# Where the load of a modulation tile stands in the queue: behind the weights of the two steps that follow it, in place of ahead of them

## Chip, cores and metric

The kernel runs on one core of a Trainium2 chip. The metric is device time in microseconds (us) of one execution; lower is better. The kernel before took 1530.79 us, the median of three runs (1523.31, 1530.79 and 1536.02).

## What is computed

One decoder block on x of 256 tokens by 2048 channels, all in float32. Six vectors of 2048 (shifts, scales and gates) come from a conditioning vector c; they are what this document calls the modulation.

```python
mod = jax.nn.silu(c) @ w_mod + b_mod            # w_mod: 2048 x 12288
sh1, sc1, g1, sh2, sc2, g2 = jnp.split(mod, 6)
h = rms_norm(x, norm1_g) * (1.0 + sc1) + sh1
q, k, v, u, gates = jnp.split(h @ w_in, split_pts)
...                                             # causal attention over q, k, v; state-space scan over u
merged = sigmoid(gate_a) * (y_attn @ w_attn_br) + sigmoid(gate_s) * (y_ssm @ w_ssm_br)
x = x + g1 * (merged @ w_out)
h2 = rms_norm(x, norm2_g) * (1.0 + sc2) + sh2
up = causal_dwconv(h2 @ w_up, conv_w, conv_b)
val, gt = jnp.split(up, 2, axis=-1)
x = x + g2 * ((silu(gt) * val) @ w_down)
```

## The kernel before

All weights stream from HBM once, as tiles of 128 x 1024 float32 (512 KB), 656 of them. Three kinds of tile share the way in:

- **Weight tiles** (464). `split_hi` (line 186, ScalarE) rounds a landed tile to a high part `whi`, `split_lo` (line 191, VectorE) takes the rest `wlo`; TensorE then multiplies with both parts. One tile is one *step* of TensorE. The block functions `chan_block` (240), `tok_block` (331) and `joint_block` (284) append the steps: 24 matmuls of 256 columns, 12 of 512, or 8 of 512 with 8 of 256. The raw tile is done with when `wlo` has been written. There are three buffers each for `whi` and `wlo` (`WB = 3`), so the split of step n+2 can begin when TensorE has finished step n-1.
- **Modulation tiles for TensorE** (76, source `in_w_m`), read by `mod_block` (451). TensorE multiplies them raw, as float32, with the conditioning vector in 32 columns (line 464, written `modp`). The raw tile is done with when TensorE has read it. In most of the program they come two at a time; this document calls two of them a *unit*.
- **Gate tiles** (116, source `in_w_g`), read by `gate_block` (490): VectorE multiplies and sums them in one instruction (line 501). The raw tile is done with after that.

The order of the work is a list, `plan`, written by the block functions and by `with_mods` (988), which weaves units and gate tiles between the weight tiles at set rates. Around the steps spoken of below, it reads: weight, weight, unit of two modulation tiles, weight, gate tile, weight, gate tile. `go` (213) walks the list: for a weight it emits the splits up to two steps ahead (`split_ahead`), for a modulation or gate tile the reading instruction. TensorE's own order follows it: the unit's matmuls stand between the two weights' steps before them and the two behind.

All loads are issued from SyncE's queue (line 124, `load_next`), in the order of the list. The raw tiles of weights, modulation and gates share five buffers (`RAW = 5`, tile `raw`), taken in rotation: a load takes the buffer of the load five places before it, and SyncE's queue stands until that tile is done with. From line 1190 on (after about 610 us) modulation and gate tiles have four buffers of their own (`mraw`), and `raw` serves weights alone.

Stages by time in the profile: up to about 60 us the first loads and the norm; to about 320 us the input projection (`w_in`: tiles `up`, `kp`, `qp`, `vp`, `gep`) with the modulation of the first sub-layer; to about 440 us more of `w_in` without modulation tiles, and attention and scan; to about 600 us the gates (`gap`) and the attention branch (`pap`) with the modulation of the second; then the rest. The state-space scan and its tables run on VectorE and ScalarE beside all of this, a piece per step.

Of the kernel before, what the change touches and what calls it, by code (L numbers as in the profile page):

```python
# [42 lines left out]
def block_kernel(ctx: ExitStack, tc: tile.TileContext, I, out):  # L43
# [57 lines left out]
    R_SET, R_SCAN, R_QK, R_ATT = 0.9, 1.05, 2.0, 2.2  # L101
    R_LAST, R_GAP, R_PAP, R_GLU, R_PPP, R_OUT, R_FFN = 1.0, 1.3, 1.3, 0.6, 0.4, 0.9, 0.34
    plan = []
    loaded = []
    place = {"load": 0}

    ring = {"w": lambda: wp.tile([128, 2, 512], F32, name="raw", tag="raw", bufs=RAW)}

# [3 lines left out]
    def ring_of(i):  # L112
        return "mod" if plan[i][0] == "m" and "mod" in ring else "w"

    def load_next():
        kind, src, _ = plan[place["load"]]
        r = ring_of(place["load"])
        held[r] += 1
        raw = ring[r]()

        if r == "mod" and "lo" in place:
            V.tensor_copy(raw[:, 0, 0:1], place["lo"][:, 0, 0:1].bitcast(F32))
        flat = raw.rearrange("p a b -> p (a b)")
        DMA.dma_start(flat, src)
        loaded.append((raw, r))
        place["load"] += 1

    behind = {}

    def after(inst, earlier):  # L130

        tc.add_manual_dep(inst.ins, earlier.ins.name,
                          mybir.DependencyInfo(mybir.DependencyClass.NoSync, mybir.DependencyReason.DATA),
                          reason="order")
# [5 lines left out]
    def unload(i):  # L140
        held[loaded[i][1]] -= 1
        loaded[i] = None

    def load_ahead():
        while place["load"] < len(plan):
            r = ring_of(place["load"])
            if held[r] >= room[r]:
                break
            load_next()

    def load_until(i):
        while place["load"] <= i and place["load"] < len(plan):
            load_next()

    bg = []
    agenda = {}
# [2 lines left out]
    def later(n, fn):  # L159
        agenda.setdefault(clock["step"] + n, []).append(fn)  # L160
# [4 lines left out]
    def run_bg():  # L165
        for entry in list(bg):
            entry[2] += entry[1]
            while entry[2] >= 1.0:
                entry[2] -= 1.0
                if next(entry[0], None) is None:  # L170
                    bg.remove(entry)
                    break
# [25 lines left out]

    def add_weights(src, fn):
        weights.append(len(plan))  # L200
        plan.append(("w", src, fn))

    def add_mod(src, fn):
        plan.append(("m", src, fn))

    def split_ahead(n):
        while done["hi"] <= n + WB - 1 and done["hi"] < len(weights):
            load_until(weights[done["hi"]])
            split_hi(weights[done["hi"]])
            split_lo(weights[done["hi"]])  # L210
            done["hi"] += 1

    def go(end=None):

        while done["plan"] < (len(plan) if end is None else end):
            i = done["plan"]
            kind, _, fn = plan[i]
            if kind == "m":
                load_until(i)
                load_ahead()  # L220
                fn(loaded[i][0])
                unload(i)
                done["plan"] += 1
                continue
            split_ahead(weights.index(i, max(0, done["hi"] - 4)))
            load_ahead()
            fn(*hi_lo.pop(i))
            for f in agenda.pop(clock["step"], []):
                f()
            run_bg()  # L230
            clock["step"] += 1
            done["plan"] += 1
# [7 lines left out]
    def chan_block(name, w, c0, kbs, act_hi, act_lo, post, k0=0, w0=None, seed=None, groups=None):  # L240
# [39 lines left out]
        for u in range(kbs):  # L280
            add_weights(wsrc(w, (w0 if w0 is not None else k0 // 2) + u, c0),
                        lambda hi, lo, u=u: step(u, hi, lo))
# [168 lines left out]
    def mod_block(part, k0, nk, finish, ps_tile, lag=0):  # L451

        st = {}
        n = 128 * nk
        per = 1024 // n

        def step(kb, raw):
            if kb == 0:
                st["p"] = ps_tile([128, n], "modp")
            raw = raw.rearrange("p a b -> p (a b)").rearrange("p (k n) -> p k n", n=n)  # L460
            for i in range(per):
                k = per * kb + i
                r0 = 32 * (k % 4)
                mm = PE.matmul(st["p"][r0:r0 + 32], cpad[:, k], raw[:, i], start=k < 4, stop=k >= 12,  # L464
                               tile_position=(0, r0))
                if "mod" in behind:
                    after(mm, behind["mod"])
                behind["mod"] = mm
            if kb == 16 // per - 1:
                rows = sm.tile([128, n], F32, name="rows", tag="rows", bufs=RB)  # L470
                A.copy(rows, st["p"])
                if lag:
                    later(lag, lambda: finish(rows))
                else:
                    finish(rows)

        at = 32 * (0, 1, 3, 4).index(part) + 8 * (k0 // 4) + 2 * (k0 % 4)
        parts = [(I["w_m"][at + kb], lambda raw, kb=kb: step(kb, raw)) for kb in range(16 // per)]

        size = max(1, 4 // per)  # L480
        return [parts[i:i + size] for i in range(0, len(parts), size)]
# [8 lines left out]
    def gate_block(part, k0, nk, dst, done=None):  # L490

        st = {}
        base = 16 * (2, 5, 0, 3).index(part)

        def step(k, half, raw):
            flat = raw.rearrange("p a b -> p (a b)")
            if k == 0 and half == 0:
                st["s"] = sm.tile([128, nk, 2], F32, name="gsum", tag="gsum")
                V.tensor_copy(st["s"].rearrange("p a b -> p (a b)"), rb[:, 0:2 * nk])
            sums = st["s"]  # L500
            V.scalar_tensor_tensor(flat, flat, 1.0, cb[:, 1024 * half:1024 * half + 1024], op0=ALU.mult,  # L501
                                   op1=ALU.mult, accum_out=sums[:, k, half:half + 1])
            if k == nk - 1 and half == 1:
                ks = slice(k0, k0 + nk)
                V.tensor_add(dst[:, ks], sums[:, :, 0], sums[:, :, 1])
                V.tensor_add(dst[:, ks], dst[:, ks], b_mod[:, 16 * part + k0:16 * part + k0 + nk])
                if done is not None:
                    done()

        return [[(I["w_g"][base + k0 + k, half], lambda raw, k=k, half=half: step(k, half, raw))]  # L510
                for k in range(nk) for half in range(2)]
# [75 lines left out]
    def mod1(k0, nk):  # L587
        def sc(rows):
            cols_of(rows, 1, k0, nk, a1)
            scale_cols(a1, norm1_g, k0, nk)  # L590
            place["a1"] = k0

        def sh(rows):
            cols_of(rows, 0, k0, nk, sh1)
            make_h(k0, nk)

        if k0 == 0:
            return mod_block(1, k0, nk, sc, m1_tile) + mod_block(0, k0, nk, sh, bu_tile)
        return woven(mod_block(1, k0, nk, sc, m1_tile), gate_block(0, k0, nk, sh1, lambda: make_h(k0, nk)))
# [405 lines left out]
    def next_mod():  # L1005
        for part in mods.pop(0):
            add_mod(*part)
# [9 lines left out]
    chunks, k0 = [], 0  # L1017
# [4 lines left out]
    mods += m0[:len(m0) // 2]  # L1022
    all_mods()
    go()
    st1 = {}
    for q in range(8):
        squares(st1, range(2 * q, 2 * q + 2), xT[q])
    norm_rows(st1, a1[:, 0:1])
    mods += m0[len(m0) // 2:]
    all_mods()  # L1030
    go()
    set_gen = setup()
    spread(set_gen, R_SET)
# [51 lines left out]
    def mod2(j):  # L1085
        lag = int(j < 3)

        def sc(rows):
            cols_of(rows, 4, 4 * j, 4, a2)
            scale_cols(a2, norm2_g, 4 * j, 4)  # L1090

        scale = mod_block(4, 4 * j, 4, sc, m1_tile, lag)
        if j < 3:
            return woven(scale, gate_block(3, 4 * j, 4, sh2))
        return scale + mod_block(3, 4 * j, 4, lambda rows: cols_of(rows, 3, 4 * j, 4, sh2), bu_tile, lag)
# [107 lines left out]
    parts = [m for j in range(1, 4) for m in gate_block(2, 4 * j, 4, g1)]  # L1203
    while parts or rest:
        mods += parts[:4] + rest[:1]
        parts, rest = parts[4:], rest[1:]
# [209 lines left out]
```

## Time and profile before

| | |
|---|---|
| median of three runs | 1530.79 us |
| the profiled execution's own time | 1532.48 us |
| its span in the profile | 1530.6 us |
| TensorE (PE) busy | 1469.6 us, 96% |
| VectorE (DVE) busy | 1110.3 us, 73% |
| ScalarE (ACT) busy | 842.0 us, 55% |
| TensorE's granted clock, mean | 0.989 |
| moved by DMA | 353.47 MB, 231 GB/s in the mean |

PE stands for TensorE's matmuls and PEld for its weight loads, which overlap them; SPq is SyncE's queue, which only issues DMAs. In a row of waits, "A <- B" says that A stood idle until B was done. Matmul ends are modelled, and a matmul's shown duration overlaps the next one's, so a busy PE is not one at its peak.

### The profile page before, as it was taken

To read this page: it belongs to the slowest core of one execution; us is meant where nothing else is said; L and a number is where in the kernel's file an instruction comes from. 1 tells how busy PE (TensorE), PEld (TensorE's weight loads), DVE (VectorE), ACT (ScalarE), POOL (GpSimd) and SP (SyncE) were. 2 spreads that over 40 slices of the span, in tenths; PEclk is the share of its full clock that TensorE was granted. 3 is DMA by queue.
4 is the path that set the end of the run, shared out by engine and by line. 5 is a ranking of instruction groups with operands and counts; after the bars stand their busy time and mean duration, and the time that the engine had idled before them with its cause. 6 is when DMAs were issued, how large, how long until landed. Compare 5 with 4: busy or idle time off the path is not lost.

```text
span 1530.6 us, 24302 instructions
## 1 busy us (share of the span) xinstructions
PE 1469.6 (96%) x9382; PEld 1236.0 (81%) x9382; DVE 1110.3 (73%) x1881; ACT 842.0 (55%) x1193; POOL 9.8 (1%) x22
## 2 busy tenths in 40 slices
PE   7989989989999899999989999999999999999998
PEld 4757767689977678788868888888888888888887
DVE  2789765986676869999578888887555667666654
ACT  3665667867675534654445555555444455555442
POOL 1000000000000000000000000000000000000000
PEclk8999999999999999999999999999999999999999
DMA  8788878733357867879576777775555555555663
GB/s 298 283 292 298 297 267 293 244 125 125 127 192 274 286 253 273 326 244 344 188 274 235 250 264 245 255 257 201 191 187 189 191 192 188 189 189 191 205 209 110
DMA packets 99110, 353.47 MB, mean 231 GB/s; under 512 B 10962, under 2 KB 13138, under 8 KB 98994
## 3 DMA queue, kind: packets, MB, share of 16 engines
q1 hardware_dynamic: 97808, 348.17, 65.7%
q0 software_dynamic: 1040, 3.61, 0.7%
q8 instruction: 73, 1.20, 0.3%
q14 instruction: 43, 0.34, 0.1%
q10 hardware_dynamic: 146, 0.15, 0.0%
HBM read 349.79 MB, written 2.10 MB: 230 GB/s over the span
## 4 chain that ended last, share of the span: by engine, by line
PE 73%; DVE 10%; DMA 9%; ACT 5%; issue 3%; SPq 0%; ACTq 0%; DVEq 0%
PE vp L302 11%; PE dp L302 10%; PE gp L302 10%; PE dp L304 5%; PE vp L304 5%; PE gp L304 5%; DVE wlo L191 4%; PE outp L302 4%; DMA raw<-in_w_in_dram 3%; ACT whi L186 3%; PE gap L302 2%; PE outp L304 2%; PE modp L464 2%; PE ppp L302 2%; DMA raw<-in_w_ga_dram 2%
## 5 line engine op out<-in xcount | busy, mean ns | idle before, releaser
L191 DVE TENSOR_TENSOR wlo<-raw,whi 128x1024 fp32r<-128x1024 f32 x464 | 566.3, 1223 | 325.4 <-ACT whi L186 323.3
L186 ACT CAST whi<-raw 128x1024 fp32r<-128x1024 f32 x464 | 486.6, 1050 | 550.4 <-PE dp L302 131.8
L302 PE MATMUL vp<-hl,whi 128*128 128x512 f32 x704 | 244.9, 393 | 1.0 <-ACT whi L186 1.0
L302 PE MATMUL dp<-g,whi 128*128 128x512 f32 x704 | 244.3, 391 | 0.0
L302 PE MATMUL gp<-hl,whi 128*128 128x512 f32 x640 | 222.3, 392 | 0.0
L304 PE MATMUL dp<-g,wlo 128*128 128x256 f32 x704 | 197.7, 281 | 0.0
L304 PE MATMUL vp<-hl,wlo 128*128 128x256 f32 x704 | 196.1, 279 | 0.0
L304 PE MATMUL gp<-hl,wlo 128*128 128x256 f32 x640 | 178.2, 278 | 0.0
L302 PEld LDWEIGHTS vp<-hl,whi 128*128 128x128 f32 x704 | 131.9, 187 | 31.1 <-issue 1.3
L302 PEld LDWEIGHTS dp<-g,whi 128*128 128x128 f32 x704 | 131.9, 187 | 28.6
L302 PEld LDWEIGHTS gp<-hl,whi 128*128 128x128 f32 x640 | 119.8, 187 | 27.0
L304 PEld LDWEIGHTS dp<-g,wlo 128*128 128x128 f32 x704 | 133.0, 189 | 0.0
L304 PEld LDWEIGHTS vp<-hl,wlo 128*128 128x128 f32 x704 | 132.6, 188 | 0.0
L304 PEld LDWEIGHTS gp<-hl,wlo 128*128 128x128 f32 x640 | 120.6, 188 | 0.0
L302 PE MATMUL gap<-hl,whi 128*128 128x512 f32 x256 | 96.4, 415 | 0.8 <-ACT whi L186 0.8
L302 PE MATMUL outp<-m,whi 128*128 128x512 f32 x256 | 91.1, 400 | 0.0
L501 DVE SCALAR_TENSOR_TENSOR raw<-raw,cb 128x1024 f32<-128x1024 f32 x60 | 73.0, 1220 | 10.7 <-DMA raw<-in_w_g_dram 9.2
L304 PE MATMUL gap<-hl,wlo 128*128 128x256 f32 x256 | 73.9, 289 | 4.5 <-DVE wlo L191 4.5
L501 DVE SCALAR_TENSOR_TENSOR mraw<-mraw,cb 128x1024 f32<-128x1024 f32 x56 | 68.2, 1221 | 12.6 <-DMA mraw<-in_w_g_dram 12.0
L304 PE MATMUL outp<-m,wlo 128*128 128x256 f32 x256 | 71.5, 280 | 0.0
L302 PEld LDWEIGHTS gap<-hl,whi 128*128 128x128 f32 x256 | 49.5, 193 | 18.8 <-ACT whi L186 3.7
L302 PEld LDWEIGHTS outp<-m,whi 128*128 128x128 f32 x256 | 48.1, 188 | 14.4 <-issue 2.9
(343 smaller groups left out, 2599.7 us busy)
## 6 DMA issues: line engine op xcount, KB each, us to landing
raw<-in_w_up_dram SPq DMA_DIRECT2D x176, 512.0 KB, 3.5
raw<-in_w_in_dram SPq DMA_DIRECT2D x96, 512.0 KB, 4.6
raw<-in_w_down_dram SPq DMA_DIRECT2D x88, 512.0 KB, 4.1
raw<-in_w_m_dram SPq DMA_DIRECT2D x68, 512.0 KB, 5.4
raw<-in_w_g_dram SPq DMA_DIRECT2D x60, 512.0 KB, 4.5
mraw<-in_w_g_dram SPq DMA_DIRECT2D x56, 512.0 KB, 5.0
raw<-in_w_ga_dram SPq DMA_DIRECT2D x32, 512.0 KB, 4.6
raw<-in_w_out_dram SPq DMA_DIRECT2D x32, 512.0 KB, 4.3
```

Source lines behind the costliest of these rows:

```text
L186: A.copy(hi, loaded[i][0])
L191: V.tensor_sub(lo, loaded[i][0], hi_lo[i][0].bitcast(F32))
L302: follow(PE.matmul(joined(p[m]), hi4[:, k, ms], joined(a), start=u == 0 and k == 0, stop=False, skip_group_check=True))
L304: PE.matmul(p[m][:, 0], lo4[:, k, ms], a[:, 0], start=False, stop=u == kbs - 1 and k == 3, skip_group_check=True)
L464: mm = PE.matmul(st["p"][r0:r0 + 32], cpad[:, k], raw[:, i], start=k < 4, stop=k >= 12, tile_position=(0, r0))
L501: V.scalar_tensor_tensor(flat, flat, 1.0, cb[:, 1024 * half:1024 * half + 1024], op0=ALU.mult, op1=ALU.mult, accum_out=sums[:, k, half:hal ...
```

## The change

Loads no longer go out in the order of the list. A new function, `see_next`, walks the list and makes the order of the loads: weight and gate tiles go into it as they come; a modulation tile for TensorE that uses the shared five buffers is put aside with a count of two (`LAG`), which every weight tile that follows takes one off; at zero it goes into the order, right behind that weight. The tiles of the first modulation block of all keep their place. Where the code needs a tile that is still put aside, `load_until` sends it at once. The order of the work on the engines is still that of the list, so far as the scheduler that places the instructions leaves it.

```diff
+    order, behind_weights = [], []
+    LAG = 2
...
+    def see_next():
+
+        i = place["seen"]
+        place["seen"] += 1
+        if plan[i][3] and ring_of(i) == "w":
+            behind_weights.append([i, plan[i][3]])
+            return
+        order.append(i)
+        if plan[i][0] == "w":
+            for entry in behind_weights:
+                entry[1] -= 1
+            while behind_weights and behind_weights[0][1] <= 0:
+                order.append(behind_weights.pop(0)[0])
+
     def load_next():
-        kind, src, _ = plan[place["load"]]
-        r = ring_of(place["load"])
+        i = order.pop(0)
+        src = plan[i][1]
+        r = ring_of(i)
...
-        loaded.append((raw, r))
-        place["load"] += 1
+        loaded[i] = (raw, r)
...
     def load_ahead():
-        while place["load"] < len(plan):
-            r = ring_of(place["load"])
+        while True:
+            while not order and place["seen"] < len(plan):
+                see_next()
+            if not order:
+                break
+            r = ring_of(order[0])
             if held[r] >= room[r]:
                 break
             load_next()
 
     def load_until(i):
-        while place["load"] <= i and place["load"] < len(plan):
-            load_next()
+        while i not in loaded:
+            if order:
+                load_next()
+            elif place["seen"] <= i:
+                see_next()
+            else:
+                order.append(behind_weights.pop(0)[0])
...
-        parts = [(I["w_m"][at + kb], lambda raw, kb=kb: step(kb, raw)) for kb in range(16 // per)]
+        wait = LAG if k0 or part > 1 else 0
+        parts = [(I["w_m"][at + kb], lambda raw, kb=kb: step(kb, raw), wait) for kb in range(16 // per)]
```

**The input projection.** SyncE's queue in the middle of it, before: two weights, the unit, then weight, gate, weight, gate. The names `raw_...` are numbers of buffers in use, handed out in order of the program; a name can stand for a different source in the other kernel.

```order
L124 DMA raw_1174<-in_w_in_dram 128x1024
L124 DMA raw_1202<-in_w_in_dram 128x1024
L124 DMA raw_1210<-in_w_m_dram 128x1024
L124 DMA raw_1212<-in_w_m_dram 128x1024
L124 DMA raw_1237<-in_w_in_dram 128x1024
L124 DMA raw_1239<-in_w_g_dram 128x1024
L124 DMA raw_1266<-in_w_in_dram 128x1024
L124 DMA raw_1268<-in_w_g_dram 128x1024
```

The same eight loads now:

```order
L143 DMA raw_1174<-in_w_in_dram 128x1024
L143 DMA raw_1202<-in_w_in_dram 128x1024
L143 DMA raw_1210<-in_w_in_dram 128x1024
L143 DMA raw_1212<-in_w_g_dram 128x1024
L143 DMA raw_1237<-in_w_in_dram 128x1024
L143 DMA raw_1239<-in_w_m_dram 128x1024
L143 DMA raw_1266<-in_w_m_dram 128x1024
L143 DMA raw_1268<-in_w_g_dram 128x1024
```

The two modulation tiles have moved from places three and four to six and seven: two weights and a gate tile have passed them. TensorE's order is the same at this place: it reads the unit between the second weight's step and the third's.

**The gates of the second stretch.** SyncE's queue where modulation tiles come back, before (`in_w_ga` are weight tiles):

```order
L124 DMA raw_4500<-in_w_ga_dram 128x1024
L124 DMA raw_4506<-in_w_m_dram 128x1024
L124 DMA raw_4508<-in_w_m_dram 128x1024
L124 DMA raw_4510<-in_w_ga_dram 128x1024
L124 DMA raw_4516<-in_w_g_dram 128x1024
L124 DMA raw_4518<-in_w_ga_dram 128x1024
L124 DMA raw_4520<-in_w_g_dram 128x1024
```

And now:

```order
L143 DMA raw_4500<-in_w_ga_dram 128x1024
L143 DMA raw_4506<-in_w_ga_dram 128x1024
L143 DMA raw_4512<-in_w_g_dram 128x1024
L143 DMA raw_4514<-in_w_ga_dram 128x1024
L143 DMA raw_4516<-in_w_m_dram 128x1024
L143 DMA raw_4518<-in_w_m_dram 128x1024
L143 DMA raw_4520<-in_w_g_dram 128x1024
```

Here, too, two weights and a gate tile have passed the unit. Further on in this stretch a few units are sent by `load_until` and stand with no weight, or one, ahead of their old place.

## Rows read from the trace of the kernel before

**Rows 1.** The page: GB/s in 40 equal slices of the span.

```profile
GB/s 298 283 292 298 297 267 293 244 125 125 127 192 274 286 253 273 326 244 344 188 274 235 250 264 245 255 257 201 191 187 189 191 192 188 189 189 191 205 209 110
```

**Rows 2.** Busy time by stretch: length, engines' busy us, PEclk, DMA share, GB/s.

```profile
60.00:295.00 235.00, 213.29 (x1216) 161.38 (x1214) 184.95 (x431) 162.41 (x255) 2.12 (x4) 0.99 0.79 283
440.00:600.00 160.00, 148.55 (x1219) 119.45 (x1217) 124.39 (x211) 75.39 (x113) 0.00 (x0) 0.97 0.76 269
```

**Rows 3.** Waits of weight loads, 60 to 295 us: total us, times, longest.

```profile
PEld qp L345 <- ACT whi L186: 10.3, 6, 3.0
PEld vp L348 <- DVE wlo L191: 5.8, 8, 1.1
PEld qp L348 <- DVE wlo L191: 4.8, 6, 1.1
PEld vp L345 <- ACT whi L186: 4.3, 3, 2.0
...
PEld modp L464 <- DMA raw<-in_w_m_dram: 2.8, 4, 1.4
PEld kp L348 <- DVE wlo L191: 2.6, 3, 1.9
```

**Rows 4.** The same waits, 440 to 600 us.

```profile
PEld gap L304 <- DVE wlo L191: 6.4, 6, 2.3
PEld gap L302 <- ACT whi L186: 3.7, 4, 1.3
PEld pap L268 <- ACT whi L186: 3.7, 3, 2.0
PEld pap L272 <- DVE wlo L191: 1.9, 3, 0.7
```

**Rows 5.** Groups of instructions, 60 to 295 us: both splits; busy, mean ns, idle before.

```profile
L191 DVE TENSOR_TENSOR wlo<-raw,whi 128x1024 fp32r<-128x1024 f32 x62 | 75.5, 1221 | 27.7 <-ACT whi L186 27.6
L186 ACT CAST whi<-raw 128x1024 fp32r<-128x1024 f32 x61 | 63.6, 1047 | 43.3 <-DMA raw<-in_w_in_dram 35.5 <-DVE tw L699 4.0 <-DVE a L526 2.0
```

**Rows 6.** Timeline, 195 to 224 us: SyncE's issues and TensorE's units; start, us.

```profile
195.48 1.10 SPq L124 DMA_DIRECT2D raw<-in_w_m_dram  x2
...
208.37 1.06 PE L464 MATMUL modp<-raw,cpad 128*32 128x512 f32 x8
...
209.46 0.33 SPq L124 DMA_DIRECT2D raw<-in_w_g_dram  x1
209.88 0.86 SPq L124 DMA_DIRECT2D raw<-in_w_in_dram  x2
210.78 2.35 SPq L124 DMA_DIRECT2D raw<-in_w_m_dram  x2
...
223.02 1.07 PE L464 MATMUL modp<-raw,cpad 128*32 128x512 f32 x8
```

**Rows 7.** The chain that ended last, 203 to 231 us: start, us, what.

```profile
204.10 0.23 PE qp L350
...
223.09 1.07 PE modp L464 x8
...
224.53 6.00 DMA raw<-in_w_in_dram
```

**Rows 8.** What SyncE's queue waited for, 60 to 295 us.

```profile
SPq L124 <- DVE wlo L191: 79.2, 38, 4.6
SPq L124 <- PE modp L464: 34.3, 12, 5.2
```

**Rows 9.** From issue to landing, 60 to 295 us: modulation tiles, then weights.

```profile
DMA to landing us min/median/max: 3.4/6.1/7.4
...
DMA to landing us min/median/max: 3.4/4.9/8.0
```

**Rows 10.** Matmuls on modulation tiles: 60 to 295 us, then 440 to 600 us.

```profile
L464 PE MATMUL modp<-raw,cpad x128: 589/593/617, 67.6 to 287.8; 128*32 128x512 f32 x128
...
L464 PE MATMUL modp<-raw,cpad x96: 592/593/617, 448.4 to 571.6; 128*32 128x512 f32 x96
```

More of the change, by code (lines that the diff above doesn't have):

```diff
@@ L103, in block_kernel @@
     plan = []
-    loaded = []
-    place = {"load": 0}
+    loaded = {}
+    place = {"seen": 0}
+    order, behind_weights = [], []
+    LAG = 2
     ring = {"w": lambda: wp.tile([128, 2, 512], F32, name="raw", tag="raw", bufs=RAW)}
@@ L200, in add_weights, with add_mod @@
         weights.append(len(plan))
-        plan.append(("w", src, fn))
-    def add_mod(src, fn):
-        plan.append(("m", src, fn))
+        plan.append(("w", src, fn, 0))
+    def add_mod(src, fn, lag=0):
+        plan.append(("m", src, fn, lag))
     def split_ahead(n):
@@ L216, in go @@
             i = done["plan"]
-            kind, _, fn = plan[i]
+            kind, _, fn, _ = plan[i]
             if kind == "m":
```

## The prediction

> **What bounds the kernel now.** I read the page first, then the busy time by stretch, then the waits inside the two stretches that the change touches, and last the timeline and the chain there. The page's line of busy times (its shares stand in the table above) has TensorE at 96% of the span, which seems to leave little; the stretches [rows 2] show where it lies. From 60 to 295 us and from 440 to 600 us, the stretches in which modulation tiles share the five buffers with the weights, matmuls cover 213.29 of 235 us and 148.55 of 160 us. As a matmul's end is modelled and laps over the next one's start, stalls are better read from the weight loads. In the first stretch PEld waited for `whi`, `wlo` or a modulation tile 10.3 + 5.8 + 4.8 + 4.3 + 2.8 + 2.6 = 30.6 us [rows 3]; in the second 6.4 + 3.7 + 3.7 + 1.9 = 15.7 us [rows 4]. Together 46.3 us: the purse that a better order of loads can draw on.
>
> Why are `whi` and `wlo` late? ScalarE, which makes `whi`, stood idle 43.3 us before it in the first stretch, 35.5 us of that until a `w_in` tile landed; VectorE then waited 27.6 us for ScalarE [rows 5]. So the tile comes late, and the split only passes that on. Yet the DMA engines are at 0.79 and 0.76 [rows 2]. What is late is the issue. The timeline [rows 6] shows a whole turn: a unit's two loads are issued from 195.48, TensorE reads them at 208.37 to 209.43, and only then, at 209.46, does the load five places behind go out, followed within 1.4 us by four more that had stood behind it. The next unit repeats it: issued at 210.78, read at 223.02 to 224.09. One buffer is thus held 13 to 14 us, of which a landing takes 6.1 us in the median [rows 9]. And the chain of the work that ended last [rows 7] goes just that way: the unit's matmuls at 223.09, then the load of a weight from 224.53 with 6.00 us. SyncE's queue stood 34.3 us for TensorE's reading, in 12 waits, beside 79.2 us, in 38, for `wlo` [rows 8].
>
> **The change part by part.** No instruction is added or taken away on TensorE, VectorE or ScalarE, and the number and size of the loads stay. The bookkeeping runs when the program is built and costs nothing. What moves is the issue of the modulation tiles: in a turn of eight, from places three and four to six and seven. Everything that passes them, two weights and a gate tile, is issued earlier by two places; nothing else on SyncE's queue is crossed, and no other queue.
>
> First stretch. Before, a turn is a closed loop: the unit is read, the load that needs its buffer goes out, it lands, it is split, its step and the next run, and the next unit is read. With 4.9 us for the landing [rows 9], 1.05 + 1.22 = 2.27 us for the split [rows 5], two steps of 12 matmuls at 0.23 us [rows 7] = 5.5 us and 1.07 us for the unit [rows 6], that is 13.7 us; the trace has 15 intervals between 67.6 and 287.8 us [rows 10], 14.7 us each. (128 matmuls are 16 groups of eight, the first of them a single tile.)
>
> After, the load that needs the unit's buffer is a weight five steps of the list away from being multiplied, so this loop is slack by several microseconds. What is late next is the unit itself. Call T the length of a turn, and count from TensorE's start on the step two before the unit. The second modulation tile takes the buffer of the weight five places before it, the one whose step stands right before the next unit. That weight can be issued when the fifth tile of the turn is split, and that split waits for a `whi` buffer, which TensorE frees after its first step, at 2.75 us; plus 2.27 us is 5.0 us. It lands L later, is split in 2.27 us, the modulation tile goes out and lands another L later, and must be there when TensorE has done the two steps of the next turn, at T + 5.5. So T = 1.8 + 2L, unless TensorE needs longer: four steps and a unit are 4 x 2.75 + 1.07 = 12.1 us. With 4.9 us for the weight and 6.1 us for the modulation tile [rows 9], T = 1.8 + 11.0 = 12.8 us. Against 14.7 that is 1.9 us for each of 15 turns: 28 us, a little under the 30.6 us of stalls [rows 3]. That is the upper end of this term, and I don't expect it whole: the queue stood far longer for `wlo` than for TensorE's reading, 79.2 against 34.3 us [rows 8]. If the stalls were shared out like these waits, the change would take 34.3 / 113.5 = 30% of them, 9 us, which is the lower end. VectorE is busy 184.95 of 235 us, and would be at 85% in a stretch shortened by 17 us, so some splits wait behind other work however early the tile is. I take 17 us, near the middle of 9 and 28.
>
> Second stretch. Here a unit stands every three steps, the 96 matmuls are 12 units, 11.2 us apart [rows 10], and a few units are sent without having been passed. The stalls are 15.7 us [rows 4]; 30% of them is 5 us, all of them 16 us. I take 7 us, nearer to the low end because of those units.
>
> Elsewhere: before 60 us four single modulation tiles move by a place or two among loads that are still filling empty buffers; from 0 to 1 us either way. From 610 us on the order is unchanged. The granted clock, 0.99 and 0.97 in the two stretches [rows 2], may rise where gaps close: 3% of lost clock over 160 us is at most 5 us, kept for the far end of the range alone.
>
> The cover for the later issue is the two steps that TensorE runs between landing and reading: 13 to 14 us of holding [rows 6] less 6.1 us of landing. At 283 GB/s [rows 2] one tile of 0.524 MB goes out every 1.9 us; moved by three places, the modulation tile comes 5.6 us later and still before its reading, by one to two microseconds. If that is gone, TensorE waits at the unit with two weights split and ready behind it, since it takes its work in order.
>
> Sum, against the profiled execution's 1532.48 us (1.7 us over the median of the runs, 1530.79): 1532.5 - 17 - 7 = 1508.5 us.
>
> The Trainium skill speaks against this change in "DMA: Bandwidth & Descriptors", section "Rules for kernel authors": a DMA is to be issued early, with the wait on it late, so that its fixed cost lies under work. The kernel before does that with the modulation tiles, and its trace shows the price: a tile that has landed early holds one of five buffers [rows 6]. By the rule the sum would be a loss, that of the second rival below; by the rows it is the gain above.
>
> **Rivals.** *The stalls move to the splits.* Weights land earlier, but ScalarE and VectorE don't split them earlier, being busy with scan and tables (VectorE 79% and 78% [rows 2]). For it: the many waits on `wlo` [rows 8]. Against it: ScalarE was idle until a landing in 35.5 of its 43.3 us [rows 5]. Then the low ends hold: 9 + 5 = 14 us, or less: 1519 us, say 1518 to 1531.
>
> *The unit comes too late* (the other side). By T = 1.8 + 2L the change breaks even with 14.7 us at L = 6.4 us. Above that each turn is longer than before. For it: the longest landings are 7.4 and 8.0 us [rows 9], because loads go out in bursts, and the modulation tiles' median, 6.1 us, is close to the point. Against it: that median comes from standing at the end of the bursts of rows 6, which the new order breaks up. With L = 7 us in every turn, T = 15.8: 15 x 1.1 = 17 us lost, and about half as much in the second stretch, 1532 + 25 = 1557 us.
>
> *All stalls go.* T falls to TensorE's own 12.1 us: 1532.5 - 46 = 1486 us, with up to 5 us of clock below that. Eight tiles in 12.1 us are 347 GB/s; the fastest slice of the page shows 344 [rows 1], so this is at the edge of what was ever moved.
>
> *The change does not do what it says.* In the first stretch the order of the queue shows every unit passed by two weights, so this holds for the second stretch only, in part, and is in its term.
>
> **How the numbers follow.** Forecast, a gain of 17 to 37 us (1495 to 1515): 0.48. More than that: 0.10. The first rival, 1515 to 1531: 0.25. Between 1531 and 1546, gains and late units in balance: 0.08. The second rival beyond that: 0.09. One per cent of 1530.8 is 15.3 us, about what a measurement of this kernel can tell from no change; faster than 1515.5 us is then 0.48 + 0.10, with a little of the first rival: 0.59. Slower than 1546 us is 0.09, and 0.32 lies between. For a range that holds 8 in 10 I leave out the slowest 0.10 and about half of the case of the larger gain: 1490 to 1538 us.
>
> **What would show it.** Right: SyncE's waits for PE `modp` fall from 34.3 us to a few; the time from a unit's issue to its reading falls from 13 to 14 us to about 8; units stand some 13 us apart in the first stretch; ScalarE's idle time until a `w_in` landing falls to about half; GB/s rise above 300 in both stretches. First rival: these all hold, but waits of PEld for `wlo` stay, with VectorE over 85%. Second rival: PEld `modp` waits for DMA `raw<-in_w_m` grow from 2.8 us to tens. Wrong altogether: the stretches keep their 235 and 160 us with the queue's waits merely renamed, which would mean that the five buffers were not what bounds them.

## The result, and the profile after

The changed kernel takes 1517.38 us (median of 6 runs, 1515.12 to 1523.13) beside 1534.43 us of the kernel before (6 runs on the same chip): a ratio of 0.9912, 95% interval 0.9889 to 0.9935. It is faster, by the ratio about 13.5 us where 24 were forecast (the two medians stand 17 us apart). The time lies in the predicted range and 9 us above the predicted number.

The busy times of the two stretches, in the columns of [rows 2], already say that they did not fare alike:

```profile
60.00:295.00 235.00, 213.68 (x1193) 160.88 (x1195) 182.82 (x423) 159.70 (x253) 2.13 (x4) 0.96 0.80 280
440.00:600.00 160.00, 152.34 (x1368) 125.98 (x1367) 135.87 (x227) 80.56 (x118) 0.00 (x0) 1.00 0.82 286
```

The second stretch does more in its 160 us than before: 1368 matmuls against 1219, at a granted clock of 1.00 against 0.97. The first has 1193 matmuls, fewer than the 1216 of [rows 2], and its clock has fallen from 0.99 to 0.96. Yet the waits of weight loads that [rows 3] showed there are nearly gone. These are the first stretch's after:

```profile
PEld modp L491 <- DMA raw<-in_w_m_dram: 13.4, 11, 4.4
PEld gep L295 <- ACT gep L285: 5.2, 2, 4.1
...
PEld up L295 <- ACT up L287: 3.3, 2, 2.7
...
PEld vp L372 <- ACT vp L366: 3.2, 1, 3.2
PEld qp L372 <- ACT qp L366: 2.9, 1, 2.9
...
PEld qp L375 <- DVE wlo L218: 1.6, 2, 1.4
PEld vp L375 <- DVE wlo L218: 1.1, 1, 1.1
```

Waits for `whi` and `wlo` made up 27.8 of the 30.6 us of [rows 3], and four rows that stand below those make 6.4 us more (`gep` 2.4 and 2.1, `kp` 1.0, `up` 0.9); here the two rows for `wlo` are 2.7 us and a third, of `kp`, is 0.8. In their place stand waits for the modulation tiles' own loads (13.4 us, from 2.8) and, new in kind, waits for ScalarE's copies of accumulators into PSUM (`gep`, `up`, `vp`, `qp` of lines 285, 287 and 366): 5.2 + 3.3 + 3.2 + 2.9 = 14.6 us. In the second stretch [rows 4] the 15.7 us have become small and nothing as large has come up:

```profile
PEld pap L299 <- DVE wlo L218: 2.0, 2, 1.3
...
PEld pap L295 <- ACT whi L213: 1.7, 2, 0.8
```

What the change was made to do, it does. Against [rows 5], both splits from 60 to 295 us:

```profile
L218 DVE TENSOR_TENSOR wlo<-raw,whi 128x1024 fp32r<-128x1024 f32 x60 | 73.2, 1221 | 25.4 <-ACT whi L213 25.2
...
L213 ACT CAST whi<-raw 128x1024 fp32r<-128x1024 f32 x59 | 61.6, 1048 | 31.6 <-DMA raw<-in_w_in_dram 13.5 <-DVE raw L529 6.6 <-DVE wlo L218 3.2
```

ScalarE waits 13.5 us for weights to land, where it was 35.5. And against [rows 6], a unit's two loads on SyncE's queue, then TensorE's reading of that unit and of the next:

```profile
197.73 2.65 SPq L143 DMA_DIRECT2D raw<-in_w_m_dram  x2
...
204.02 1.05 PE L491 MATMUL modp<-raw,cpad 128*32 128x512 f32 x4 [0.32 <-DMA raw<-in_w_m_dram]
205.26 1.05 PE L491 MATMUL modp<-raw,cpad 128*32 128x512 f32 x4 [0.18 <-DMA raw<-in_w_m_dram]
217.34 1.05 PE L491 MATMUL modp<-raw,cpad 128*32 128x512 f32 x4
```

From the issue to the start of the reading it is 6.3 us (197.73 to 204.02) and to its end 8.6 (206.31), where [rows 6] have 12.9 and 13.95. The unit is also read otherwise than before: its two loads go out 2.3 us apart (two of 0.33 us each within 2.65), where they went out 0.8 us apart (within 1.10), and TensorE takes each tile by itself, four matmuls in 1.05 us and four in 1.05 us more. In [rows 6] the eight of a unit ran together in 1.06 us. SyncE's waits, against [rows 8]:

```profile
SPq L143 <- DVE wlo L218: 95.3, 45, 7.0
...
SPq L143 <- PE modp L491: 16.1, 13, 2.8
```

The queue's waits for TensorE are 18.2 us less, but those for `wlo` are 16.1 us more, so that the two together have hardly changed (113.5 and 111.4 us).

To see where the time came and went, take the moment at which ScalarE begins to split the n-th weight tile. In the timeline of the changed kernel this row is the 66th:

```profile
258.91 1.05 ACT L213 CAST whi<-raw 128x1024 fp32r<-128x1024 f32 x1
```

In the kernel before, the 66th began at 269.2 us, so the changed kernel stands 10.3 us ahead there. Read out in this way (us from the start of each profiled span; the last column is the 464th and last tile):

| kernel | 16th | 26th | 66th | 81st | 111th | 151st | last |
|---|---|---|---|---|---|---|---|
| before | 90.8 | 124.3 | 269.2 | 334.6 | 457.0 | 622.4 | 1518.2 |
| changed | 82.1 | 124.4 | 258.9 | 335.6 | 456.7 | 610.0 | 1506.3 |
| changed, again (e12) | 81.1 | 123.4 | 258.8 | 334.7 | 455.1 | 607.4 | 1502.4 |
| e1, order kept | 80.4 | 118.9 | 253.8 | 329.7 | 450.8 | 605.4 | 1506.9 |
| e9, order kept, narrower | 80.5 | 119.2 | 252.6 | 329.7 | 450.2 | 606.2 | 1505.2 |
| e2, last two at once | 81.8 | 122.8 | 258.3 | 329.1 | 449.0 | 600.8 | 1498.3 |
| e3, both edits | 80.2 | 117.8 | 251.7 | 321.6 | 442.5 | 594.8 | 1494.1 |
| e11, both edits, again | 79.2 | 118.7 | 250.4 | 320.4 | 441.3 | 595.9 | 1494.4 |
| e10, both edits, narrower | 82.5 | 122.4 | 255.6 | 325.2 | 446.1 | 606.3 | 1498.9 |
| e5, second stretch alone | 87.3 | 122.3 | 266.6 | 329.9 | 450.8 | 604.7 | 1505.6 |
| e6, first stretch alone | 81.0 | 123.3 | 256.5 | 330.8 | 453.4 | 614.3 | 1516.0 |

The first two rows tell the story. The changed kernel is 8.7 us ahead at the 16th tile, level at the 26th, 10.3 ahead at the 66th, and 1.0 behind at the 81st: the first stretch's gain is made and then given back whole, in two parts of it. The second stretch's is kept: 12.4 us at the 151st tile, 12 at the end.

**The first place, 72 to 118 us.** TensorE's order has changed there, though the diff says nothing of TensorE. The scheduler that places the instructions put the first matmul of the next block between the two tiles of a unit, presumably because it expects the modulation tiles later now; its reasons were not traced. The order of the changed kernel:

```
L377 MATMUL kp<-whi,hl 128x512
L491 MATMUL modp<-raw,cpad 32x512 x2
L372 MATMUL qp<-whi,hl 128x512
L491 MATMUL modp<-raw,cpad 32x512 x2
L372 MATMUL kp<-whi,hl 128x512
```

The block `qp` starts on an accumulator that ScalarE copies into PSUM. On the chip:

```profile
72.19 1.05 PE L491 MATMUL modp<-raw,cpad 128*32 128x512 f32 x4
75.19 0.50 PE L372 MATMUL qp<-whi,hl 128*128 128x512 f32 x1 [1.95 <-ACT qp L366]
75.62 1.17 PE L491 MATMUL modp<-raw,cpad 128*32 128x512 f32 x4
```

TensorE stood 1.95 us at the one `qp` matmul, with the unit's second tile and the whole step of `kp` queued behind it. The Trainium skill says why nothing passes it ("PSUM — Partial Sum Buffer", section "Engine vs sequencer instructions": matmuls start and complete in program order); the trace agrees, the second tile's matmuls begin 0.43 us after `qp`. After it the granted clock falls to the lower of its two levels (1.2 GHz; the stretch from 76 to 80 us, below, has 0.57 in the mean), and the chain's pieces stand 0.43 us apart, where at a clock of 1.00 they are 0.23:

```profile
75.19 0.50 PE qp L372
75.69 1.10 PE modp L491 x4
76.79 0.73 PE kp L372
77.52 0.43 PE kp L375
77.94 0.43 PE kp L377
```

The busy times of that stretch and of one after the second place (below):

```profile
76.00:80.00 4.00, 4.00 (x12) 2.62 (x9) 3.96 (x26) 0.00 (x0) 0.00 (x0) 0.57 1.02 383
289.30:294.00 4.70, 4.68 (x12) 2.01 (x13) 4.47 (x8) 1.69 (x7) 0.00 (x0) 0.50 0.79 263
```

It happens again with `vp` at 86.94 us (2.30 us of standing) and `gep` at 99.82 us (3.20). The waits for `up` are of another kind: they stand at the start of a block, not within a unit, and remain in e1 and e3, where the order is kept (2.6 us in both from 60 to 125 us).

**The second place, 280 to 291 us.** The first stretch's last unit is the 43rd and 44th modulation tile. The description of the kernel says that buffers are taken in rotation, five places before; that does not hold for every load. Here the build gave the 44th tile the 43rd's own buffer. The chain of the changed kernel:

```profile
280.15 4.57 DMA raw<-in_w_m_dram
284.71 0.04 issue
284.76 1.08 PE modp L491 x4
285.84 0.02 issue
285.85 3.42 DMA raw<-in_w_m_dram
289.27 0.04 issue
289.32 1.92 PE modp L491 x4
```

The load goes out 0.02 us after TensorE has read the tile before it, so TensorE waits for a whole landing (3.51 us of standing in the timeline), and the matmuls behind the wait run at a granted clock of 0.50: four in 1.92 us, where four took 1.08 before it.

### The profile page after: what moved, and what is told of

It reads as the page before. It is cut to its first block, busy times and chain, and to the rows that moved or that the text cites. A ratio compares the mean times of both kernels' runs of the same rounds, so it can differ in the third digit from the quotient of the medians.

```text
span 1518.6 us, 24307 instructions
## 1 busy us (share of the span) xinstructions
PE 1463.7 (96%) x9382; PEld 1237.9 (82%) x9382; DVE 1109.5 (73%) x1881; ACT 842.0 (55%) x1193; POOL 9.8 (1%) x22
## 4 chain that ended last, share of the span: by engine, by line
PE 74%; DVE 10%; DMA 6%; ACT 5%; issue 3%; POOL 0%; SPq 0%; ACTq 0%; DVEq 0%
PE dp L329 11%; PE vp L329 10%; PE gp L329 10%; PE dp L331 6%; PE vp L331 5%; PE gp L331 5%; PE outp L329 4%; DVE wlo L218 4%; ACT whi L213 2%; PE outp L331 2%; PE modp L491 2%; PE ppp L329 2%; PE gap L329 2%; DMA raw<-in_w_m_dram 2%; DMA raw<-in_w_g_dram 2%
## 5 line engine op out<-in xcount | busy, mean ns | idle before, releaser
L329 PE MATMUL gap<-hl,whi 128*128 128x512 f32 x256 | 92.7, 403 | 0.0
L329 PE MATMUL outp<-m,whi 128*128 128x512 f32 x256 | 90.8, 399 | 0.0
L529 DVE SCALAR_TENSOR_TENSOR raw<-raw,cb 128x1024 f32<-128x1024 f32 x60 | 73.1, 1219 | 22.0 <-DMA raw<-in_w_g_dram 21.5
L491 PE MATMUL modp<-raw,cpad 128*32 128x512 f32 (+1 forms) x320 | 53.9, 573 | 7.4 <-DMA raw<-in_w_m_dram 6.7
```

Source lines behind the costliest of these rows:

```text
L329: follow(PE.matmul(joined(p[m]), hi4[:, k, ms], joined(a), start=u == 0 and k == 0, stop=False, skip_group_check=True))
```

## The experiments

Four kernels first, for the two places. **e1** forbids TensorE's build order to cross steps; no semaphore and no instruction is added:

```diff
     def follow(inst):
+        if "step" in behind:
+            after(inst, behind.pop("step"))
...
+                    end = PE.matmul(p[:, t], act_lo(kk)[:, ts], hi[:, k], start=False, ...
+            behind["step"] = end
```

(and so in the two other forms of a step, and for a modulation tile's first matmul). TensorE's rows then differ from the changed kernel's only at the three places near 72, 84 and 96 us, and a little from about 590 us on.

> Edit: the changed kernel, with TensorE's matmuls of two neighbouring steps of the list kept in the order of the list (an order edge, no semaphore); TensorE's rows differ from the changed kernel's at three places near 72, 84 and 96 us, where a unit of modulation tiles is no longer split by matmuls of the following block. My theory: these split units are what gives back most of the first stretch's gain (PE waits of 2.5 to 3.8 us for ScalarE's seed copies, then matmuls 0.43 instead of 0.23 us apart), so the weights at the 25th step are used about 8 us sooner and the time is 5 to 9 us below the changed kernel's (ratio to before 0.985 to 0.988). Rival (the first stretch ends on the splits or the scan whatever TensorE's order): within 2 us of the changed kernel (ratio 0.990 to 0.993). Rival (the units come too late in general): no change either, and waits of PE for the seed copies replaced by waits for the tiles' DMAs.

Measured: 0.9889 (0.9834 to 0.9944). That lies between the expectation and its first rival, and the time of whole runs does not tell them apart. The profile shows the place mended: the 26th tile begins at 118.9 instead of 124.4 us, and 4.6 us are still there at the 151st (2.0 against the changed kernel's repeat). The other rival came true in part: TensorE's waits from 60 to 125 us for modulation tiles' loads rose from 0.5 to 4.9 us, in place of 7.4 us for `qp`, `vp` and `gep`.

**e2** loads the last two tiles of the first stretch's last unit at once:

```diff
+        first = part == 4 and k0 == 0
-        parts = [(..., wait) for kb in range(16 // per)]
+        parts = [(..., 0 if first and kb > 5 else wait) for kb in range(16 // per)]
```

> Edit: the changed kernel, with the last two tiles of the first stretch's last unit (the 43rd and 44th modulation tiles) loaded at once rather than behind two weights. In the built kernel this puts the 44th tile into a buffer that was read five loads earlier, where the changed kernel put it into the 43rd's own. My theory: the changed kernel's wait of PE for that DMA near 286 to 290 us (3.5 us) and the half clock after it go, so 3 to 8 us less than the changed kernel (ratio to before 0.986 to 0.989). Rival (what follows, the scan and attention, waits for the splits or for VectorE there): within 2 us of the changed kernel (0.990 to 0.993).

Measured: 0.9891 (0.9843 to 0.9939). TensorE reads the unit without a wait (two of its eight matmuls at 275.55 us, six together here):

```profile
282.75 1.06 PE L491 MATMUL modp<-raw,cpad 128*32 128x512 f32 x6
```

From the 66th to the 81st tile it takes 70.8 us, where the changed kernel took 76.7. In the time, the ratio is 0.002 below the changed kernel's, about 3 us, which lies within the interval, and between what was expected and the rival.

**e3** has both edits, and **e4** is the changed kernel with one line edited. e4's TensorE rows have none of the three split units, as e3's, but they are not e3's throughout: near 63, 108 and 230 us e4 reads a part of a unit a step or two before the rest. So the lag differs, and a little of the order with it:

```diff
-    LAG = 2
+    LAG = 1
```

> Edit: both of the two edits together. My theory: the two give-backs are independent places and their gains add: 8 to 15 us below the changed kernel, about 1505 us where before is 1532 (ratio 0.980 to 0.986). Rivals that hold for one place only: the better of the two alone. If neither place matters: 0.990 to 0.993.

> Edit: the changed kernel with the modulation tiles behind one weight rather than two. TensorE's rows and the buffers come out as in the third kernel of this call (both edits together), so against that one only the order of the loads differs. My theory (the order of the buffers coming free is what counts, and a unit in the list stands two steps behind its weights): behind one weight half of the crossing is left, so 3 to 8 us above the third kernel (ratio to before 0.985 to 0.990). Rival (two weights are too late, units are awaited): at or below the third kernel, and waits of PE for the modulation tiles' DMAs shorter than its.

Measured: e3 1504.36 us, 0.9824 (0.9778 to 0.987); e4 1513.4 us, 0.9875 (0.9823 to 0.9928). Mended at both places, the first stretch keeps its gain: 13.0 us ahead of before at the 81st tile, 27.6 at the 151st. Both ratios lie where they were expected. Behind one weight, the weights are late again, as PEld's waits from 60 to 295 us show:

```profile
PEld qp L375 <- DVE wlo L218: 6.7, 5, 2.9
...
PEld kp L375 <- DVE wlo L218: 3.5, 3, 2.3
```

Then which stretch pays, whether the order alone would do, and whether later is better still. **e5** and **e6** lag the units of one stretch only:

```diff
-        wait = LAG if k0 or part > 1 else 0
+        wait = LAG if k0 and part > 1 else 0                (e5)
+        wait = LAG if (k0 > 0) != (part > 1) else 0         (e6)
```

> Edit: the changed kernel with the wait behind two weights for the units of the second stretch (440 to 600 us) alone; the first stretch's units are loaded as in the kernel before, and TensorE's rows there are those of the kernel before. My theory (the first stretch's gain is given back, the second's is kept): all of the changed kernel's gain, 9 to 15 us below before (ratio 0.990 to 0.994). By the prediction's own terms (17 us of the first stretch, 7 of the second): 5 to 9 us below before (0.994 to 0.997).

> Edit: the changed kernel with the wait for the first stretch's units (60 to 295 us) alone; the second stretch as in the kernel before. My theory: within 4 us of before (ratio 0.997 to 1.003), with the weights at the 65th step about 10 us sooner than before and at the 80th no sooner. By the prediction's own terms: 13 to 21 us below before (0.986 to 0.992).

Measured: e5 1516.08 us, 0.9897 (0.9866 to 0.9928); e6 1529.82 us, 0.9984 (0.9964 to 1.0004). So the second stretch alone gives all that the change gives, and the first alone next to nothing, about as expected and against the prediction's own terms, though e6 is 12.7 us ahead of before at the 66th tile. (Of e5's lead in its profile, 4.7 us stand at the 81st tile already, where its loads are those of before: the scatter from one profile to another, of which more below.) The waits of 440 to 600 us agree, e5 first, then e6, whose loads there are those of before:

```profile
PEld py L865 <- DVE w L916: 3.9, 2, 2.2
...
PEld pap L299 <- DVE wlo L218: 2.5, 3, 1.4
```

```profile
PEld gap L331 <- DVE wlo L218: 6.4, 5, 2.8
PEld pap L299 <- DVE wlo L218: 4.3, 6, 1.4
PEld pap L295 <- ACT whi L213: 3.6, 4, 1.1
```

**e7** is e1's edit on the kernel before; **e8** is e3 with `LAG = 3`.

> Edit: the kernel before (its loads in the order of the list) with TensorE's order of neighbouring steps kept as in the first kernel of the call before. My theory: in the kernel before PE waits for loads at those places anyway, so the order alone is worth little: within 5 us of before (ratio 0.997 to 1.003). Rival (the strict order is what made the third kernel of the call before fast, whatever the loads): 8 to 15 us below before (0.990 to 0.995).

> Edit: the kernel with both edits (TensorE's order kept, the last two tiles of the first stretch loaded at once), its units behind three weights rather than two. My theory: behind two weights the crossing is undone already, behind three the buffers come free out of turn again and some units are awaited: 1 to 10 us above the kernel with two (ratio to before 0.984 to 0.990), with waits of PE for the modulation tiles' DMAs longer than its. Rival (the later the better, as from one to two weights): 4 to 9 us below it (0.977 to 0.980).

Measured: e7 1538.34 us, 1.0041 (1.002 to 1.0062), 6.3 us slower than before by the ratio, just outside the 5 us that I had allowed: kept order is worth nothing without the new order of loads, and this rival is out. e8 1522.2 us, 0.9928 (0.9906 to 0.9951), by the ratios 16 us above e3, more than I had expected. Its waits from 60 to 295 us, and below them e3's:

```profile
PEld modp L496 <- DMA raw<-in_w_m_dram: 27.4, 23, 3.4
```

```profile
PEld modp L496 <- DMA raw<-in_w_m_dram: 14.8, 13, 2.9
```

Behind three weights the units are what is awaited. One, two and three weights: 0.9875, 0.9824, 0.9928. That three is worse than two is clear, also against e3's repeat below (0.9865). That one is worse than two rests on e3 and e4 beside each other (1502.34 to 1508.30 us against 1510.76 to 1514.53, four runs each) and on the kind of wait; the repeat, on another chip, is only 0.001 below e4.

**e9** and **e10** keep TensorE's order only while modulation tiles are to come (the line `behind["step"] = end` stands under `if any(entry[0] == "m" for entry in plan[done["plan"]:])`), without and with e2's edit, in more runs.

> Edit: the changed kernel with TensorE's order of neighbouring steps kept, as in the first experiment, but only as long as modulation tiles are still to come, so that TensorE's rows after the modulations stay nearer to the changed kernel's; more rounds than there. My theory: the split units cost 5 to 7 us of the time at 72 to 118 us, and nothing later gives that back: ratio to before 0.986 to 0.989. Rival (the next wait, that for the 44th modulation tile near 285 us, takes it): ratio 0.990 to 0.993.

> Edit: the same and the last two tiles of the first stretch loaded at once (the two edits together, the order kept only while modulation tiles are to come). My theory: as the third experiment, 10 to 15 us below the changed kernel, 1500 to 1507 us where before is 1531 (ratio 0.979 to 0.984). Rival (the third experiment's result was partly its later order of TensorE): 0.984 to 0.988.

Measured: e9 0.9916 (0.9892 to 0.9939), e10 0.9875 (0.9849 to 0.9902). Both came out on the rivals' side. e9 repeats e1's profile (119.2 at the 26th tile, 329.7 at the 81st), so the places are mended there too, and still the whole run gains nothing over the changed kernel; the rival that I had named, the wait for the 44th tile, does not take it, since e9 is 5.9 us ahead of the changed kernel at the 81st tile. Where it goes is told below. e10 has e3's order on TensorE and VectorE up to about 580 us and is nevertheless 3.6 us behind it at the 81st tile and 11.5 at the 151st; only the last 3 or so of these are in a part that is ordered otherwise. So one profile against another is good to some 4 us at 330 us, and to 8 at 590.

**e11** and **e12** repeat e3 and the changed kernel, side by side.

> No new edit: the kernel of the third experiment (both edits) once more, beside the changed kernel on the same chip, with more rounds. If both edits are worth what the third experiment showed: 1500 to 1508 us, ratio to before 0.979 to 0.986. If the tenth experiment's number is the truer one: 1509 to 1514 us, 0.986 to 0.989. In the profiles so far TensorE's 512-column matmuls at 820 to 1050 us followed each other after a mean of 230, 231.5 to 232 or 236 to 237 ns, the level being set at the wait near 800 to 815 us; the third experiment's profile had 236.7. If the level belongs to the program, this profile has 236 to 237 again; if it belongs to the execution, it may have another.

> No edit: the changed kernel once more, for comparison with the one beside it. Ratio to before 0.989 to 0.9935 as measured first; its first profile had the 512-column matmuls at 820 to 1050 us 230 ns apart: again 230 if the level belongs to the program, perhaps another if it belongs to the execution. My theory of the two give-backs: 8 to 15 us above the kernel with both edits, with the same places in its trace (PE waiting for seed copies near 72 to 110 us, for the 44th modulation tile near 286 us).

Measured: e11 1509.17 us, 0.9865 (0.9843 to 0.9886); e12 1517.99 us, 0.9925 (0.9903 to 0.9947). On one chip, the kernel with both edits is 8.8 us below the changed kernel, with intervals that don't touch, and its profile repeats e3's to within 1.4 us in every column of the table. It is the best version of this study: 20.6 us below before in e11, 26 in e3.

## Why the prediction was right, and where its sizes were not

**The loop was right in what it undid, not in what holds it now.** From the 26th to the 66th tile, ten turns, a turn took 14.5 us before (144.9 us / 10) and 13.45 after (134.5 / 10), where the steps had 14.7 and 12.8. The 17 us taken for 15 turns were 1.1 us a turn; measured is 1.0. The signs named for it came: issue to reading 6.3 to 8.6 us ("about 8"), units 13.3 us apart (204.02 to 217.34), ScalarE's wait for landings down to 13.5 of 35.5 us. SyncE's waits for TensorE's reading fell only from 34.3 to 16.1 us, not to "a few", and the GB/s stayed below 300 in the mean of both stretches, though they rose above it in these ten turns. Their busy times, before and then after, in the columns of [rows 2], and below them the matmuls and weight loads of modulation tiles alone (PE, PEld, ACT):

```profile
124.30:269.20 144.90, 133.15 (x766) 102.13 (x766) 102.02 (x177) 95.00 (x145) 2.12 (x4) 1.00 0.80 285
124.40:258.90 134.50, 130.07 (x713) 100.67 (x711) 102.84 (x178) 90.70 (x120) 2.13 (x4) 1.00 0.88 312
```

```profile
124.30:269.20 144.90, 10.63 (x72) 1.54 (x72) 1.17 (x2) 1.00 0.80 285
124.40:258.90 134.50, 14.72 (x72) 2.20 (x72) 1.17 (x2) 1.00 0.88 312
```

TensorE is now busy 130.07 of the 134.5 us, 97%, so a turn can hardly get shorter while TensorE has this work: it is 13.0 us a turn as the profile counts it, where the steps had 12.1. Part of the difference is a term that the steps left at 1.07 us, the unit. Read in two halves it takes TensorE longer, and the same 72 matmuls cover 14.72 us instead of 10.63 at a granted clock of 1.00 in both. "No instruction is added" did not mean that none gets dearer.

**The step that failed** is "No instruction is added or taken away on TensorE, VectorE or ScalarE", priced at nothing. No instruction was; but TensorE's order and the choice of buffers moved with the loads, and each undid a part, beside the dearer units. In the table, 26th tile: 123.5 us in the mean of the four kernels that lag the first stretch's units behind two weights and have the split units (changed, e12, e2, e6), 119.4 in the five with the order kept (e1, e9, e3, e11, e10). From the 66th to the 81st: 76.0 us in the mean of the five with the 44th tile in the 43rd's buffer (changed, e12, e1, e9, e6), 70.1 in the four without (e2, e3, e11, e10). The two groups do not overlap at either place (122.8 to 124.4 and 117.8 to 122.4; 74.4 to 77.1 and 69.6 to 70.9). 4.1 + 5.9 = 10 us, about the difference between e11 and e12; of the 20 us that the changed kernel gives back between the 16th and the 26th tile (8.8) and between the 66th and the 81st (11.3), it is half. In the changed kernel the first stretch's term of 17 us came to 0. With both places mended it is 9 to 14 us at the 81st tile, and e3, e10 and e11 (1504.36, 1512.08 and 1509.17 us) lie about the forecast of 1508.5 us. That is partly luck: the first stretch gives them 9 to 14 us where 17 were taken, the second 5 to 13 where 7 were.

**Part of the 17 us was perhaps never there.** From the 16th to the 26th tile before took 33.5 us; with the order kept it takes 37.6 to 39.9, starting earlier. VectorE is nearly full in that part, which the mean over the stretch (79%) had hidden. From 60 to 125 us, before and then e3:

```profile
60.00:125.00 65.00, 57.03 (x338) 43.28 (x337) 57.86 (x208) 46.26 (x66) 0.00 (x0) 0.97 0.83 298
60.00:125.00 65.00, 57.00 (x340) 42.77 (x339) 59.50 (x206) 46.92 (x66) 0.00 (x0) 1.00 0.86 298
```

VectorE is busy 57.86 and 59.50 of 65 us, 89% and 92%. That is what "some splits wait behind other work however early the tile is" would look like. But TensorE itself waits there in e3 for modulation tiles and for `up`, and for no `wlo`:

```profile
PE modp L496 <- DMA raw<-in_w_m_dram: 5.4, 6, 2.5
PE up L297 <- ACT up L289: 2.6, 2, 2.3
```

That these tiles are late because VectorE frees their buffers late (SyncE waits 18.0 us for `wlo` in this part of e3, 10.8 before) is argued, not shown.

**The second stretch was mis-sized the other way.** The term was 7 us, near the low end "because of those units" that are not passed. From the 111th to the 151st tile it is 165.4 us before and 153.3 after, 12.1 us; over all kernels, 164.0 in the mean of the three with the old loads there (before, e6, and e7 with 165.8) and 154.3 in the mean of the nine with the new behind two weights (151.8 to 160.2): 9.7 us. That is inside the bounds of 5 and 16; the middle would have been nearer. The clock, kept for the far end, did rise from 0.97 to 1.00.

**Before 60 us** the term was "from 0 to 1 us either way". At the 4th tile, 38.0 us before, the nine kernels with the first stretch's units behind two weights are 2.5 to 5.1 us ahead (e5 1.0, e7 1.5); at the 11th, 60.3 us before, it is 0.0 to 4.0 and e7 has 2.6, so what is left then lies within the scatter.

**The range.** It was wide enough to hold the first rival too, and of the sum's two terms one came to 0 for 17 and the other to some 10 to 12 for 7. That the time fell into the range says little for the sum.

**The rivals.** The first named almost the measured time (1519), for another reason: its sign, waits for `wlo` that stay, did not come. The second rival, units too late, is what the changed kernel would have become with one more weight: in e8 TensorE's weight loads wait 27.4 us for modulation tiles. Of that sign the changed kernel has some, 13.4 us from 2.8. The Trainium skill's rule ("DMA: Bandwidth & Descriptors", section "Rules for kernel authors": issue early, wait late) is borne out by the trace of e8 and these 27.4 us. From none to two weights the runs go against it (ratios of 0.9875 for one, 0.9824 and 0.9865 for two): there the buffer that a landed tile holds costs more than the early issue saves. "All stalls go" did not come.

**Open.** What the order alone (e1, e9) is worth in whole runs was not resolved: 0.9889 and 0.9916 against 0.9912 and 0.9925 of the changed kernel. Why the first stretch's end costs 70 us from the 66th to the 81st tile even when mended, where before took 65.4, was not tried. Nor was a kernel that keeps each unit's two loads together, which would show what the halved units cost.

## What to carry to other kernels

A change to the order of loads can change each engine's order of work and each load's buffer, although no line of the program says so: compare both before putting a price on it, above all where an in-order engine could meet the first instruction of a block that still waits for its accumulator. Read a gain off at several points along the work and not only at the end, since a gain can be made and given back within one stretch. And a term that stands for many turns is to be multiplied only by the turns in which the same thing is the bound.

## What was not expected of the hardware

From about 835 to 1035 us TensorE runs the same matmuls, 512 columns and 256 in turn, without a gap and at a granted clock of 1.00 in every kernel. Yet the 512-column ones lead to the next after a mean of 230 to 232 ns in some kernels and 236 to 237 in others, and the 256-column ones after 115 to 117 in both. The two kernels run side by side, e11 and then e12, one block by its shapes from 820 to 1050 us (the mean duration of one, in ns, stands behind the busy time):

```profile
L332 PE MATMUL gp<-hl,whi 128*128 128x512 f32 x293 | 103.8, 399 | 0.0
...
L334 PE MATMUL gp<-hl,wlo 128*128 128x256 f32 x293 | 82.3, 281 | 0.0
```

```profile
L329 PE MATMUL gp<-hl,whi 128*128 128x512 f32 x320 | 111.2, 394 | 0.0
...
L331 PE MATMUL gp<-hl,wlo 128*128 128x256 f32 x320 | 88.6, 277 | 0.0
```

Before TensorE's last wait, which falls between 797 and 828 us, every kernel is near the upper level; some leave it at that wait, the others only between about 1035 and 1065 us. It costs about 5 us: e3 is 29.1 us ahead of before at the 201st tile (741.9 against 771.1) and 24.2 at the 301st (1041.8 against 1066.0). Six kernels' profiles have the upper level (e1, e3, e5, e6, e8, e9), the repeat e11 of e3 has it too, and the changed kernel and its repeat have the lower; so it goes with the program in the two cases that were run twice. (Within the lower level the repeat differs: 230.0 and 116.7 ns in the changed kernel, 231.7 and 115.0 in e12, the same 346.7 for the pair.) It is where e1's and e9's lead over the changed kernel went in their profiles. Its cause is open.
